# Group 0's mix loaded by whole feature tiles into the operand's low part, split there, and queued ahead of the residual

## The chip, the cores and the metric

The kernel runs on one core of a Trainium2 chip. The metric is the device time of one execution in microseconds (us). A core has five engines with queues of their own: TensorE (PE in the profile: matmuls; PEld: its weight loads), VectorE (DVE), ScalarE (ACT), GpSimd (POOL) and SyncE (SP). SyncE computes nothing here; it issues nearly all of the kernel's transfers (DMAs), in the order of its queue. Each engine works through its queue in order, and an instruction that waits holds up what stands behind it.

## What is computed

One layer of a streaming encoder for 1024 prompt frames and 32 sample frames, in float32. The input is modulated, projected to three groups of heads (mLSTM, FoX attention, gMLP), and their outputs are put side by side; this is the *mix*, 1024 features for each frame. It is projected once more, added to the residual and normalised; then comes a SwiGLU FFN with a second norm:

```python
mix = jnp.concatenate([hm.reshape(B, S, D_MLSTM).astype(dt),
                       hf.reshape(B, S, D_FOX).astype(dt), hg], axis=-1) @ w_o
x = _layer_norm(ALPHA * x + (1 + g1) * mix, ln1_g, ln1_b)
h = x * (1 + sc2) + sh2
y = (jax.nn.silu(h @ w_gate) * (h @ w_up)) @ w_down
x = _layer_norm(ALPHA * x + (1 + g2) * y, ln2_g, ln2_b)
```

## The kernel before

Everything is kept with features on the 128 partitions and frames along the free axis, so 1024 features are 8 feature tiles, counted k = 0 to 7. Frames fall into group 0 (frames 0 to 511) and group 1 (512 to 1055, the sample frames last). Large products are made in three passes to keep float32 precision: every operand is split into a high part, rounded to the type that TensorE takes at full rate (`F32R`), and a low part, the rest. `gemm` (lines 111 to 119) issues high x high, high x low and low x high into one PSUM bank. Making the split costs a cast on ScalarE and a subtraction, mostly on VectorE.

The mixers write their outputs to a scratch tensor in DRAM, `dmix[c]`, laid out as partition, feature tile, frame. In group 0, mLSTM writes tiles 0 and 1 (line 636, a store for each 128 frames), FoX tiles 2 to 5 (line 777, half a tile for each head), gMLP tiles 6 and 7 (line 669). The last mLSTM block and the last FoX head of group 0 end shortly before the output projection begins.

`run` then closes the mixers' SBUF pools and opens three others in their place (lines 1347 to 1351): `ph` with the operand tiles `ah` (high) and `al` (low), each 8 x 512 values a partition; `pz` with the residual `z0`, just as large; and `p2` with small work tiles, among them a ring `tmp` of four buffers of 272 values. By the sizes of the tiles in the closed pools, `al` lies over FoX's last key and query tiles, its values, its probabilities and one buffer of transposed probabilities; `z0` lies over the other transposed probabilities, FoX's output tiles and the start of the mLSTM tiles; `p2` over mLSTM tiles. A tile can be written when the tiles it lies over have been read for the last time.

The steps around the change, in the order of the source:

1. Line 1353, `wo_res(0)`: eight loads of the residual, one for each k, 128x512.
2. Line 1355, `wo_mix(0, KORDER[:6])`: the mix's tiles 2, 3, 4, 5, 0, 1. For each half of the group (frames 0 to 255, then 256 to 511) and each k: a load of 128x256 into a `tmp` buffer (line 932), a cast into `ah` (line 934), a subtraction into `al` (line 935).
3. Lines 1360 to 1368: the gMLP projections (`tm_unit`) and two q/k units (`fm_unit`, line 1368) for group 1; both kinds store their results to DRAM from SyncE.
4. Line 1370, `wo_mix(0, KORDER[6:])`: tiles 6 and 7, in the same way.
5. Lines 1374 and 1375, `wo(0, ...)`, once for each half: eight output blocks m of 24 matmuls. Each block loads a 128x1024 piece of `w_o` and splits it (lines 102 to 106); its products take the k in the order 2, 3, 4, 5, 0, 1, 6, 7. `sublayer_end` adds the product to the residual (line 975) and gathers the sums for the norm; after block 0 it also makes a pivot that later blocks need. Three PSUM banks (`pg`) serve these blocks.
6. Lines 1377 and 1378, the norm (`ln1`), which overwrites `ah` and `al` with the FFN's operand; lines 1379 and 1380, four more q/k units, which need nothing of the projection; then the FFN and, between its parts, the mixers of group 1.

The program is not issued in the order of the source. A scheduler places each instruction in its engine's queue by its own estimate of times, with the source's order as priority; an instruction whose inputs and buffers are ready may go ahead of earlier ones that wait. It draws up the order of the whole program at once (line 1576).

Of the kernel before, what the change touches and what calls it, by code (L numbers as in the profile page):

```python
# [10 lines left out]
ALU = mybir.AluOpType  # L11
# [54 lines left out]
def f(ap):  # L66
    return ap.bitcast(F32)


class Kernel:  # L70
# [855 lines left out]
    def wo_mix(self, c, ks):  # L926
        self.phase = f"wo{c}"
        nc = self.nc
        for a, b in MM[c]:
            for k in ks:  # L930
                r = self.t(self.p2, [P, 272], F32, "tmp", 4)[:, :b - a]
                self.load(r, self.dmix[c][:, k, a:b])
                h = self.hh[c][a][:, k, :b - a]
                nc.scalar.copy(h, r)
                nc.vector.tensor_tensor(self.hl[c][a][:, k, :b - a], r, f(h), ALU.subtract)
# [309 lines left out]
    def run(self):  # L1245
        nc, tc, d = self.nc, self.tc, self.d
# [103 lines left out]
        self.pz = self.pool("pz")  # L1350
        self.p2 = self.pada = self.pool("p2")
        self.hh, self.hl, self.z = {}, {}, {}
        self.wo_res(0, self.pz)
        self.operand(0, self.ph)
        self.wo_mix(0, self.KORDER[:6])
        def tail_ada():
            for u in rest:
                self.ada(u, self.wp, "raw", RAW, self.pg, "g")

        for i in range(4):  # L1360
            if i == ADAPOS:
                tail_ada()
            self.tm_unit(w2[3 + i % 2], 256, (self.evac_gv, self.evac_gmlp)[i % 2], range(4 * (i // 2), 4 + i // 2 * 5),
                         nc.gpsimd if GENG[i] else nc.vector)
        if ADAPOS == 4:
            tail_ada()
# [101 lines left out]
        for half, (a, b) in enumerate(LN[1][::-1]):  # L1468
# [6 lines left out]
            else:  # L1475
                h, l = (self.t(pb, [P, KT * 272], F32R, f"{x}{a}", 1) for x in ("ah", "al"))
# [111 lines left out]
```

## Time and profile before

| | us |
|---|---|
| runs of the kernel | 1397.95, 1398.54 (median), 1400.02 |
| the profiled execution | 1397.36 |
| its span, first to last instruction | 1395.6 |
| TensorE busy | 1346.8 |
| VectorE busy | 1034.0 |
| ScalarE busy | 641.6 |
| GpSimd busy | 258.7 |

The profile is one execution. In its lists, `out<-in` names the tiles an instruction writes and reads; a tile has the name of the stage that was being written when it was made, so the residual of group 0 is called `mlstm_z`, the operand's parts `mlstm_ah` and `mlstm_al`, the ring `wo_tmp`, and the scratch tensor `start_dmix`. `SPq` lines are issues of transfers in SyncE's queue: the time is that of the issue, not of the transfer. A row of waits reads: who waited, for whom, us in total, times, the longest. A row of a stretch reads: its bounds, its length, the busy time (with the count of instructions) of TensorE, its weight loads, VectorE, ScalarE and GpSimd, then the granted TensorE clock, the share of the DMA engines' time and the GB/s moved. A row of a group reads: line, engine, operation, tiles, shapes, count, busy us, mean ns of one, and the idle time of the engine ahead of them with what ended it. A row of the timeline reads: start, length, engine, line, instruction, count, and in brackets the idle time before it.

### The profile page before, as it was taken

The numbers are of one execution on the slowest core, as the hardware profiler recorded it, in microseconds if no ns is written. First come the engines' busy times: TensorE is split into PE (matmuls) and PEld (weight loads), VectorE is DVE, ScalarE is ACT, GpSimd is POOL, SyncE is SP. The second block draws the span as 40 slices with busy tenths as digits, with TensorE's granted clock in tenths as the row PEclk, the third lists the DMA queues.
The fourth block names the chain that finished last, engine by engine and source line by source line (L and its number), as shares of the span: only waits on it lengthen the run. The fifth ranks groups of instructions, "written<-read, shape, count | busy, mean of one in ns | idle before, by whom it ended". The sixth has DMA issues, their size and how long they took to land.

```text
span 1395.6 us, 25879 instructions
## 1 busy us (share of the span) xinstructions
PE 1346.8 (97%) x9651; PEld 1238.7 (89%) x9651; DVE 1034.0 (74%) x2198; ACT 641.6 (46%) x1257; POOL 258.7 (19%) x292
## 2 busy tenths in 40 slices
PE   7999999999979799999999999999999999999996
PEld 4899988899979778888887889899999999999996
DVE  5548646678779657777776766678997988888777
ACT  3313234445445444545544445344673544545355
POOL 0103200052146500000000000264620000000341
PEclk9999999999999899999999999999999999999998
DMA  9764577585755656444443342555597767563321
GB/s 360 255 219 134 171 234 210 176 253 168 225 174 158 186 174 178 128 131 138 137 131 85 100 119 83 198 153 139 157 237 202 204 174 199 149 174 112 101 91 65
DMA packets 134709, 233.09 MB, mean 167 GB/s; under 512 B 22436, under 2 KB 77356, under 8 KB 134584
## 3 DMA queue, kind: packets, MB, share of 16 engines
q1 hardware_dynamic: 129272, 221.34, 51.3%
q0 software_dynamic: 5168, 9.96, 4.6%
q8 instruction: 76, 1.25, 0.4%
q14 instruction: 49, 0.40, 0.1%
q10 hardware_dynamic: 144, 0.14, 0.0%
HBM read 197.50 MB, written 53.81 MB: 180 GB/s over the span
## 4 chain that ended last, share of the span: by engine, by line
PE 68%; DVE 4%; DMA 3%; issue 1%; ACT 1%; SPq 0%; POOL 0%; DVEq 0%; ACTq 0%
PE up_g L117 5%; PE up_g L118 5%; PE up_g L119 5%; PE dn_g L119 4%; PE dn_g L117 4%; PE dn_g L118 4%; PE sup_u L119 3%; PE sup_u L117 3%; PE sup_u L118 3%; PE wo_g L117 2%; PE wo_g L118 2%; PE wo_g L119 2%; PE sup_g L118 2%; PE sup_g L119 2%; PE sup_g L117 2%; PE fox_t L753 2%
## 5 line engine op out<-in xcount | busy, mean ns | idle before, releaser
L117 PE MATMUL up_g<-mlstm_ah,up_whi 128*128 128x512 f32 (+1 forms) x384 | 142.4, 371 | 4.3 <-ACT lna_tmp L996 3.4
L118 PE MATMUL up_g<-mlstm_al,up_whi 128*128 128x512 f32 (+1 forms) x384 | 142.8, 372 | 0.6 <-DVE mlstm_al L1001 0.6
L119 PE MATMUL up_g<-mlstm_ah,up_wlo 128*128 128x512 f32 (+1 forms) x384 | 142.2, 371 | 0.0
L284 PE MATMUL tm_g<-tm_whi,start_h1l 128*128 128x256 f32 (+1 forms) x384 | 110.0, 287 | 0.0
L282 PE MATMUL tm_g<-tm_whi,start_h1h 128*128 128x256 f32 (+1 forms) x384 | 109.6, 287 | 0.0
L283 PE MATMUL tm_g<-tm_wlo,start_h1h 128*128 128x256 f32 (+1 forms) x384 | 109.5, 286 | 0.0
L117 PE MATMUL fm_g<-start_h1h,fm_whi 128*128 128x256 f32 (+2 forms) x344 | 101.9, 301 | 4.7 <-DVE fm_qkl L367 2.0
L118 PE MATMUL fm_g<-start_h1l,fm_whi 128*128 128x256 f32 (+2 forms) x344 | 101.6, 295 | 0.2 <-DVE start_h1l L223 0.2
L119 PE MATMUL fm_g<-start_h1h,fm_wlo 128*128 128x256 f32 (+2 forms) x344 | 100.8, 294 | 0.0
L1120 ACT CAST sup_whi<-sup_raw 128x1024 fp32r<-128x1024 f32 x54 | 56.0, 1048 | 90.3 <-PE dn_u L118 46.7
L117 PEld LDWEIGHTS up_g<-mlstm_ah,up_whi 128*128 128x128 f32 x384 | 74.2, 193 | 16.6 <-ACT mlstm_ah L1000 3.5
L118 PEld LDWEIGHTS up_g<-mlstm_al,up_whi 128*128 128x128 f32 x384 | 74.3, 193 | 12.6 <-DVE up_actl L1054 0.8
L119 PEld LDWEIGHTS up_g<-mlstm_ah,up_wlo 128*128 128x128 f32 x384 | 74.4, 194 | 10.7
L105 ACT CAST up_whi<-up_raw 128x1024 fp32r<-128x1024 f32 x50 | 52.4, 1049 | 62.0 <-PE dn_g L118 22.5
L726 ACT ACTIVATE fox_p<-fox_s,fox_fmx 128x384 f32<-128x384 f32 (+2 forms) x96 | 55.1, 579 | 50.6 <-DVE fox_fmx L724 43.9
L1121 DVE TENSOR_TENSOR sup_wlo<-sup_raw,sup_whi 128x1024 fp32r<-128x1024 f32 x54 | 68.1, 1265 | 10.5 <-ACT sup_whi L1120 10.5
L117 PEld LDWEIGHTS fm_g<-start_h1h,fm_whi 128*128 128x128 f32 x344 | 65.4, 192 | 10.3 <-issue 2.9
L282 PEld LDWEIGHTS tm_g<-tm_whi,start_h1h 128*128 128x128 f32 x384 | 72.3, 189 | 1.9 <-issue 1.2
L106 DVE TENSOR_TENSOR up_wlo<-up_raw,up_whi 128x1024 fp32r<-128x1024 f32 x50 | 67.1, 1341 | 9.2 <-ACT up_whi L105 8.5
L284 PEld LDWEIGHTS tm_g<-tm_whi,start_h1l 128*128 128x128 f32 x384 | 72.3, 188 | 1.5 <-issue 1.2
L117 PE MATMUL dn_g<-up_acth,dn_whi 128*128 128x512 f32 (+2 forms) x200 | 73.5, 368 | 0.0
L118 PE MATMUL dn_g<-up_actl,dn_whi 128*128 128x512 f32 (+2 forms) x200 | 73.3, 368 | 0.0
(591 smaller groups left out, 4592.9 us busy)
## 6 DMA issues: line engine op xcount, KB each, us to landing
up_raw<-w_gu SPq DMA_DIRECT2D x50, 512.0 KB
dn_raw<-w_dn SPq DMA_DIRECT2D x28, 512.0 KB
ada_late<-w_ada SPq DMA_DIRECT2D x24, 512.0 KB
wo_raw<-w_o SPq DMA_DIRECT2D x24, 512.0 KB
sup_raw<-w_gu SPq DMA_DIRECT2D x20, 512.0 KB
start_dp<-w_gu SPq DMA_DIRECT2D x19, 512.0 KB
start_dp<-w_gu POOLq DMA_DIRECT2D x19, 512.0 KB, 7.9
sup_raw<-start_dp SPq DMA_DIRECT2D x18, 512.0 KB
```

Of the source, the lines that this page charges most:

```text
L105: nc.scalar.copy(hi[:, :w], raw[:, :w])
L106: (eng or nc.vector).tensor_tensor(lo[:, :w], raw[:, :w], f(hi[:, :w]), ALU.subtract)
L117: nc.tensor.matmul(ps, hi, xh(k), start=start and k == 0, stop=False)
L118: nc.tensor.matmul(ps, hi, xl(k), start=False, stop=False)
L119: nc.tensor.matmul(ps, lo, xh(k), start=False, stop=stop and k == n - 1)
L282: nc.tensor.matmul(ps[:, :ncol], xh, hi, start=k == 0, stop=False)
L283: nc.tensor.matmul(ps[:, :ncol], xh, lo, start=False, stop=False)
L284: nc.tensor.matmul(ps[:, :ncol], xl, hi, start=False, stop=k == 7)
L726: nc.scalar.activation(pr[:, lo:hi], banks[x][:, :hi - lo], AF.Exp, bias=mxs[:, 0:1], accum_out=sums[:, x:x + 1])
L753: nc.tensor.transpose(ps[:, c:c + P], probs[y][:, b * P:(b + 1) * P], self.ident)
L1120: nc.scalar.copy(h, x)
L1121: tt(l, x, f(h), ALU.subtract)
```

## The change

`wo_mix` gets a path of its own for group 0. For each k it loads the whole 128x512 tile into the slice of `al` that will hold its low part, casts from there into `ah`, and subtracts in place, so that `al` holds the low part afterwards. Both halves of the group are views of the same two tiles, so the projection reads them as before. The `tmp` ring is no longer used by group 0's mix; sixteen loads of 128x256 become eight of 128x512, and sixteen casts and subtractions become eight of each. The path of group 1 is untouched. In `run`, the residual's eight loads move behind the first six tiles of the mix.

```diff
@@ -926,6 +926,13 @@
     def wo_mix(self, c, ks):
         self.phase = f"wo{c}"
         nc = self.nc
+        if c == 0:
+            for k in ks:
+                h, l = self.hh[0][0][:, k], self.hl[0][0][:, k]
+                self.load(f(l), self.dmix[0][:, k])
+                nc.scalar.copy(h, f(l))
+                nc.vector.tensor_tensor(l, f(l), f(h), ALU.subtract)
+            return
         for a, b in MM[c]:
             for k in ks:
                 r = self.t(self.p2, [P, 272], F32, "tmp", 4)[:, :b - a]
@@ -1350,9 +1357,9 @@
         self.pz = self.pool("pz")
         self.p2 = self.pada = self.pool("p2")
         self.hh, self.hl, self.z = {}, {}, {}
-        self.wo_res(0, self.pz)
         self.operand(0, self.ph)
         self.wo_mix(0, self.KORDER[:6])
+        self.wo_res(0, self.pz)
         def tail_ada():
             for u in rest:
                 self.ada(u, self.wp, "raw", RAW, self.pg, "g")
```

`f` views a tile as plain float32, and `load` issues a transfer from SyncE's queue.

## The prediction

> **What bounds the kernel now.** I read the page's head first, then the table of waits of TensorE over the whole run, then busy times by stretch around the wait that the change touches, then the queue of SyncE.
>
> ```profile
> span 1395.6 us, 25879 instructions
> PE 1346.8 (97%) x9651; PEld 1238.7 (89%) x9651; DVE 1034.0 (74%) x2198; ACT 641.6 (46%) x1257; POOL 258.7 (19%) x292
> ```
>
> TensorE is busy 1346.8 of 1395.6 us, so it sets the end, and only its 48.8 us of idle time, with its slow matmuls, can be won. Which idle time is the change's? The waits of TensorE, longest first:
>
> ```profile
> PE ada_t L179 <- DMA ada_araw<-w_ada: 6.7, 2, 6.3
> PE wo_g L117 <- ACT mlstm_ah L934: 5.5, 1, 5.5
> ...
> PE wo_g L117 <- DVE mlstm_z L975: 1.3, 1, 1.3
> ...
> PE wo_g L119 <- DVE wo_wlo L106: 0.7, 1, 0.7
> ```
>
> The longest is the start of the kernel. The second longest, 5.5 us in one piece, is the output projection of group 0 waiting for line 934, which makes the high part of the mix. That is the line the change replaces. Around it, by stretch (us; then PE, weight load, DVE, ACT, POOL busy, granted clock, DMA share, GB/s):
>
> ```profile
> 379.10:386.10 7.00, 6.81 (x56) 6.56 (x55) 3.95 (x7) 2.84 (x7) 1.06 (x2) 1.00 0.95 291
> 386.10:391.30 5.20, 0.00 (x0) 0.00 (x0) 0.77 (x2) 1.11 (x4) 0.00 (x0) 0.67 0.64 222
> 391.30:394.60 3.30, 3.19 (x15) 3.19 (x16) 1.59 (x5) 1.21 (x5) 0.00 (x0) 0.50 0.32 84
> 394.60:401.10 6.50, 4.52 (x31) 3.86 (x31) 5.92 (x7) 3.71 (x5) 3.22 (x3) 0.99 0.46 144
> 386.10:401.10 15.00, 7.71 (x44) 7.06 (x45) 8.28 (x13) 6.02 (x11) 3.22 (x3) 0.77 0.49 158
> 401.10:441.00 39.90, 39.89 (x327) 39.74 (x328) 35.69 (x44) 20.57 (x34) 28.27 (x26) 1.00 0.60 179
> ```
>
> The last row is the undisturbed pace: 39.90 / 327 = 0.122 us for a matmul. The 44 matmuls of 386.1 to 401.1 would take 44 x 0.122 = 5.4 us; they took 15.0. So 15.0 - 5.4 = 9.6 us is everything that can be won here: 5.2 of standstill, 3.3 - 15 x 0.122 = 1.5 at half clock behind it, and 6.5 - 31 x 0.122 = 2.7 while the pipeline starts again (9.4 by parts; boundaries cut a record or two).
>
> Why is line 934 late? The queue of SyncE, in which every load and store of this stage goes out in order:
>
> ```profile
> 331.08 0.38 SPq L91 DMA_DIRECT2D start_dmix<-tm_gms  x1
> ...
> 345.28 0.35 SPq L87 DMA_DIRECT2D wo_raw<-w_o  x1
> ...
> 360.50 0.50 SPq L91 DMA_DIRECT2D start_dmix<-fox_fr  x1
> 361.97 0.37 SPq L91 DMA_DIRECT2D start_dmix<-mlstm_mixs  x1
> 362.84 3.67 SPq L87 DMA_DIRECT2D mlstm_z<-xT  x8
> 366.61 2.82 SPq L87 DMA_DIRECT2D wo_tmp<-start_dmix  x4
> ...
> 373.85 0.88 SPq L87 DMA_DIRECT2D wo_tmp<-start_dmix  x2
> ...
> 378.76 1.02 SPq L87 DMA_DIRECT2D wo_tmp<-start_dmix  x2
> ...
> 385.39 0.91 SPq L87 DMA_DIRECT2D wo_tmp<-start_dmix  x2
> 386.39 0.47 SPq L91 DMA_DIRECT2D o_kT<-fm_qkr  x1
> 386.96 4.82 SPq L87 DMA_DIRECT2D wo_tmp<-start_dmix  x4
> ```
>
> Eight residual loads go first. Then the mix comes in 16 pieces through a ring of four buffers (`tmp`): four at once, and every further pair only when the split of an earlier pair has freed its buffers. The last four pieces, which hold tiles 6 and 7, go out at 386.96, though their data was stored by 331.08 + 0.38. The chain of waits says the same:
>
> ```profile
> 366.61 5.51 DMA wo_tmp<-start_dmix
> ...
> 378.76 5.68 DMA wo_tmp<-start_dmix
> ...
> 386.96 3.97 DMA wo_tmp<-start_dmix
> ```
>
> A round of the ring costs a landing of 4.0 to 5.7 us, and TensorE, with three blocks begun in its three banks, can do no more without tiles 6 and 7.
>
> **The change, part by part.** *The ring goes.* A tile of 128x512 now lands in its own slice of `al`, so no load waits for a split. Each load waits for two things instead. One is that `al`'s place is free: it lies over buffers of the mixers' pool (the tail of FoX's keys and queries, its values, its probabilities and one transposed block), whose last reader is the last product of FoX head 7. The other is that its tile was stored.
>
> ```profile
> SPq L87 <- DMA start_dmix<-fox_fr: 0.4, 1, 0.4
> ...
> 358.17 0.46 PE L770 MATMUL fox_o<-fox_pth,fox_v 128*128 128x512 f32 x1
> 379.17 0.38 PE L117 MATMUL wo_g<-mlstm_ah,wo_whi 128*128 128x256 f32 x1
> ```
>
> So `al` is free at 358.17 + 0.46 = 358.6. Tiles 2, 3 and 4 (earlier heads), and 6 and 7, were stored before that. Tile 5 needs the store of 360.50. The residual, whose place lies over that store's source, waited for it (the first row) and started at 362.84, so such a store takes 2.3 us. Tiles 0 and 1 need the store of 361.97: 361.97 + 2.3 = 364.3. The first product that wants the mix starts at 379.17, and TensorE is busy without a gap until then.
>
> *Order past the residual.* At worst nothing lands early and all eight mix loads and eight residual loads are in the queue from 364.3: 16 x 0.262 MB = 4.2 MB. The rate of a full queue is in this row (share 0.99, 342 GB/s):
>
> ```profile
> 365.00:370.00 5.00, 5.00 (x43) 4.98 (x42) 3.03 (x5) 3.67 (x6) 0.00 (x0) 1.00 0.99 342
> ```
>
> 4.2 / 0.342 = 12.3 us, so the residual, now last, is in at 376.6. The eight mix loads, 2.1 MB, are in at 370.4. What is late next is the residual; its first use is the end of block 0, 24 matmuls after 379.17, at 382.1. Slack 5.5 us, so I cost the move at nothing. If that cover were gone, TensorE could still begin two more blocks in its other banks (2 x 24 x 0.122 = 5.9 us) before it stood.
>
> *Issue.* 16 issues become 8. Six of them now stand ahead of the eight residual issues (3.67 us), and ahead of what is queued after those: a gMLP store and load, and the stores of the two q/k units that TensorE runs until 379. Before, twelve of the sixteen mix loads stood among these and waited for buffers. The SP wait that is added, up to 364.3 for tiles 0 and 1, holds the residual 1.5 us longer than 362.84; nobody waits for that, by the slack above.
>
> *Splits.* Whole tiles were never split in this stage; the nearest rows are the same cast and subtraction on 128x512 in the FFN of group 1.
>
> ```profile
> L934 ACT CAST mlstm_ah<-wo_tmp 128x256 fp32r<-128x256 f32 x16 | 6.0, 405 | 13.9 <-DMA wo_tmp<-start_dmix 13.8
> L935 DVE TENSOR_TENSOR mlstm_al<-wo_tmp,mlstm_ah 128x256 fp32r<-128x256 f32 x16 | 7.9, 527 | 9.1 <-ACT mlstm_ah L934 9.1
> ...
> L1120 ACT CAST sup_w2h<-sup_w 128x512 fp32r<-128x512 f32 x18 | 11.0, 609 | 0.8 <-DMA sup_w<-w_gu 0.6 <-PE sup_u L118 0.2
> ...
> L1121 DVE TENSOR_TENSOR sup_w2l<-sup_w,sup_w2h 128x512 fp32r<-128x512 f32 x18 | 12.3, 682 | 0.0
> ```
>
> ScalarE: 16 x 0.405 = 6.5 us become 8 x 0.609 = 4.9. VectorE: 16 x 0.527 = 8.4 become 8 x 0.682 = 5.5. That the subtraction works in place has no row; bounds are 0.68 (as those rows) and 1.05 (two of the half-sized ones), at most 3 us over eight, and I take 0.68. Neither engine bounds here, so the path gets nothing from it directly. But ScalarE stood 13.8 us in front of these casts, with the casts of the projection's weights behind them in its queue; that frees the weights for blocks 1 to 3, and the 2.7 us of restart go with it.
>
> *The sum.* 5.2 + 1.5 + 2.7 = 9.4 us at most. I take 9.0, keeping 0.4 for the pivot of block 0 (the wait on line 975 above), which is part of any start. The rest of the run is TensorE-bound and slides forward. Against the profiled execution (1397.36 us, its span 1395.6) that is 1388.4; the median of the runs lies 1.2 above that execution, at 1398.54, so 1389.5 us.
>
> **The rivals.**
>
> *Half-way: the tiles still come late (1394.5 us).* DMA engines were 0.95 busy up to 386.1, and six pieces, 6 x 0.131 = 0.79 MB, had still to move. If the engines had been full whatever the order, these would take 0.79 MB / 0.291 = 2.7 us, with 1.3 us of split behind them: a hole of 4.0 us instead of 5.2. Of such a hole the half clock stays too, and the gain is 1.2 + 2.7 = 3.9, 1394.5 us. Is a hole that short punished? This trace has one:
>
> ```profile
> 472.23 0.36 PE L117 MATMUL up_g<-mlstm_ah,up_whi 128*128 128x256 f32 x1 [3.35 <-ACT lna_tmp L996]
> 474.00:478.00 4.00, 3.88 (x23) 3.68 (x22) 1.23 (x4) 3.02 (x9) 4.00 (x10) 0.67 0.61 161
> ```
>
> After 3.35 us of standstill the clock fell to 0.67, so holes from there up pay. The Trainium skill ("TensorE: Matmul & The Clock Gate", section "HAM oscillation — how this bites in real kernels") asks that TensorE never idle longer than about 3.4 us; by that alone this rival, with its hole cut to 3 us by splits that overlap, would keep full clock and gain 1.5 us more, while the trace puts the border at 3.35 or below. Against the rival: three to five tiles can move from 358.6 on, when the mixers' transfers are over.
>
> *The order is kept (1397.5 us).* The program's scheduler could leave the loads of tiles 6 and 7 behind the last store of the q/k units (386.39), as now. Then they land about when they do now, and only the 1 us of two further pieces is saved. Against: the projection's weights, which the source loads later still, were issued at 345.28, so the scheduler does draw loads forward once their buffer is free.
>
> *Slower (1402 us): the cover of the first norm is spent.* Four q/k units cover the norm after the projection:
>
> ```profile
> 436.00:463.00 27.00, 25.46 (x192) 24.57 (x192) 2.98 (x6) 3.36 (x7) 1.00 0.49 147
> ```
>
> Each is 25.46 / 4 = 6.4 us. The whole order after 345 us is drawn up anew, and if the scheduler puts units ahead of the projection, TensorE has less to do during the norm, and every unit so moved uncovers 6.4 us. From 9.0 / 6.4 = 1.4 units on it costs more than the change wins; with two it is 12.7 - 9.0 = 3.7 us slower, 1402 us. For it: the units' inputs are ready all along. Against: the source puts them behind the projection and the norm, and a mix that is ready sooner leaves fewer gaps to fill with them.
>
> **How the numbers follow.** Forecast 0.55, 1389.5 us, with its own range 1386 to 1392.5 (all 9.6 won, the run like the fastest of those shown, and some luck of order, to 6 won). Half-way 0.15. Order kept 0.10. Slower 0.20. The bound of what can be told apart is 0.2%, 2.8 us: faster is below 1395.7, slower above 1401.3. So faster 0.70, same 0.10, slower 0.20. The range 1386 to 1400 holds all but the slower case.
>
> **What would show it.** In the changed profile: eight mix loads, no line 932 loads of group 0 in `tmp`, most issued before the residual and several between 358 and 365; the wait of the projection's products on the high part gone; TensorE busy from 345 to about 450 with clock 1.00; the norm's start near 427 instead of 436. The sum is wrong if a wait on the residual or on weights stands where the mix's stood. The step to the end is wrong if the norm starts 9 us sooner and the kernel doesn't end so. Half-way shows as a hole of 3 to 4 us near 386, the order kept as loads of tiles 6 and 7 behind the last q/k store, the slower case as q/k units ahead of the projection and idle TensorE during the norm.

## The result, and the profile after

Medians of the runs: 1399.88 us before (1397.53 to 1401.07, 8 runs), 1389.95 us after (1384.43 to 1395.11, 8 runs). The ratio is 0.9934, with an interval of 0.9914 to 0.9953. The changed kernel, measured again later beside the kernel before (run e8 below), gave 1388.72 against 1396.87 us, 0.9943 (0.9922 to 0.9964). The forecast was 1389.5 us.

The profiled execution of the changed kernel took 1389.64 us. The head of its page, for comparison with 1346.8 busy of a span of 1395.6 us before:

```profile
span 1387.8 us, 25846 instructions
PE 1344.1 (97%) x9651; PEld 1236.2 (89%) x9651; DVE 1030.4 (74%) x2190; ACT 641.0 (46%) x1249; POOL 260.2 (19%) x292
```

TensorE's idle time fell from 48.8 to 43.7 us, its busy time by 2.7 us (in this stage no matmul runs at a low clock any more). The same stretches as before the change, in the same columns:

```profile
379.10:386.10 7.00, 7.00 (x56) 6.70 (x56) 4.59 (x9) 3.14 (x5) 0.97 (x2) 1.00 1.00 312
386.10:391.30 5.20, 5.20 (x46) 5.20 (x44) 3.85 (x5) 3.02 (x6) 4.59 (x7) 1.00 0.89 295
...
386.10:401.10 15.00, 15.00 (x128) 15.00 (x127) 13.65 (x16) 8.03 (x13) 14.07 (x14) 1.00 0.67 210
```

Where 44 matmuls ran in 15.0 us, 128 run now, at clock 1.00. SyncE's queue after (issues, with their times):

```profile
360.81 0.37 SPq L91 DMA_DIRECT2D start_dmix<-mlstm_mixs  x1
361.27 2.80 SPq L87 DMA_DIRECT2D mlstm_al<-start_dmix  x6
364.12 6.35 SPq L87 DMA_DIRECT2D wo_z<-xT  x8
370.93 0.38 SPq L91 DMA_DIRECT2D start_dmix<-tm_gms  x1
371.61 0.33 SPq L87 DMA_DIRECT2D tm_gvn<-start_dvn  x1
...
372.93 0.32 SPq L87 DMA_DIRECT2D mlstm_al<-start_dmix  x1
...
374.31 0.32 SPq L87 DMA_DIRECT2D mlstm_al<-start_dmix  x1
...
375.60 0.49 SPq L87 DMA_DIRECT2D wo_raw<-w_o  x1
...
376.67 0.94 SPq L87 DMA_DIRECT2D wo_raw<-w_o  x2
```

(`wo_z` is the residual, `mlstm_z` before.) Six tiles go out ahead of the residual, tiles 6 and 7 at 373 and 374 instead of 387, and three loads of `w_o` right behind them. The residual's eight issues take 6.35 us where they took 3.67, though they need nothing of the mix. SyncE's own waits from 355 to 400 us say what held them:

```profile
SPq L87 <- DMA mlstm_al<-start_dmix: 2.5, 3, 1.2
```

Three of them stood until an earlier transfer, a mix tile, had landed; what makes them wait is taken up at e9. TensorE's waits from 345 to 475 us:

```profile
PE ada_g L179 <- DVE up_sil L1059: 4.1, 1, 4.1
PE up_g L117 <- DVE fm_qkl L367: 2.7, 1, 2.7
PE fm_g L117 <- ACT tm_gms L665: 1.4, 1, 1.4
```

The wait on the high part is gone. A small new one is there: line 665, gMLP's copy out of its bank, now stands in ScalarE's queue behind four of the new casts. The splits cost what the rows of the other stage had said: 0.616 us a cast (0.609 in the prediction), 0.684 us for the subtraction in place (0.68). Both rows give shortest/median/longest in ns:

```profile
L933 ACT CAST mlstm_ah<-mlstm_al x8: 602/616/622, 365.0 to 378.3; 128x512 fp32r<-128x512 f32 x8
L934 DVE TENSOR_TENSOR mlstm_al<-mlstm_al,mlstm_ah x8: 668/684/693, 365.9 to 379.8; 128x512 fp32r<-128x512 f32 x8
```

**A measure that is sharper than the time.** Single executions of one kernel differ by 10.7 us (the range above) and by up to 14.3 (the kernel before, beside e9 to e12: 1390.44 to 1404.72), more than the change is worth. Much of that lies outside the stage. Up to gMLP's third store (358.37 in the queue of before) the program has the same instructions in the same order on every engine in all the kernels of this study, and yet that store came between 356.9 and 363.0 us in the fourteen profiled executions. So each kernel's stage is measured from that store in its own trace, to the last matmul of the output projection. One execution each, in us:

| kernel | first output product | last output product | median of runs, ratio (interval) |
|---|---|---|---|
| before | 20.8 | 77.5 | 1399.88, 1397.53, 1396.87, 1397.65 |
| changed | 22.2 | 69.2 | 1389.95, 0.9934 (0.9914 to 0.9953) |
| changed, again (e8) | 21.8 | 69.2 | 1388.72, 0.9943 (0.9922 to 0.9964) |
| e1 order only | 20.6 | 75.1 | 1394.13, 0.9981 (0.9966 to 0.9996) |
| e2 whole tiles only | 21.6 | 69.5 | 1390.04, 0.9949 (0.9931 to 0.9967) |
| e3 ring of eight | 24.4 | 78.2 | 1395.16, 0.9980 (0.9962 to 0.9998) |
| e4 changed, `qkl` 3 | 22.0 | 68.9 | 1390.11, 0.9943 (0.9923 to 0.9963) |
| e5 pieces in place | 22.7 | 77.2 | 1396.27, 0.9996 (0.9983 to 1.0008) |
| e6 whole tiles, ring | 22.7 | 75.7 | 1397.38, 0.9998 (0.9981 to 1.0015) |
| e7 late split, `qkl` 3 | 21.8 | 68.7 | 1389.74, 0.9942 (0.9922 to 0.9962) |
| e9 pieces, mix early | 24.5 | 73.4 | 1393.34, 0.9963 (0.9944 to 0.9981) |
| e10 pieces, weights early | 26.7 | 74.8 | 1393.98, 0.9973 (0.9959 to 0.9988) |
| e11 pieces, both early | 24.5 | 72.7 | 1394.43, 0.9976 (0.9960 to 0.9991) |
| e12 whole tiles, both early | 23.3 | 69.8 | 1393.17, 0.9966 (0.9950 to 0.9982) |

Two executions of the changed kernel agree within 0.1 us in the last product (0.4 in the first), where their times differ by 3.7 us; of every other kernel there is one trace. The stage became 8.3 us shorter (77.5 to 69.2), which is the gain of the medians (9.9 and 8.2 us) within their spread.

### The profile page after: what moved, and what is told of

Same layout as the page of the kernel before. It is cut to its first block, busy times and chain, and to the rows that moved or that the text cites. A ratio compares the mean times of both kernels' runs of the same rounds, so it can differ in the third digit from the quotient of the medians.

```text
span 1387.8 us, 25846 instructions
## 1 busy us (share of the span) xinstructions
PE 1344.1 (97%) x9651; PEld 1236.2 (89%) x9651; DVE 1030.4 (74%) x2190; ACT 641.0 (46%) x1249; POOL 260.2 (19%) x292
## 4 chain that ended last, share of the span: by engine, by line
PE 69%; DVE 4%; DMA 2%; ACT 1%; issue 1%; POOL 0%; SPq 0%; DVEq 0%; ACTq 0%
PE up_g L117 5%; PE up_g L118 5%; PE up_g L119 5%; PE dn_g L119 4%; PE dn_g L117 4%; PE dn_g L118 4%; PE sup_u L119 3%; PE sup_u L117 3%; PE sup_u L118 3%; PE wo_g L118 2%; PE wo_g L119 2%; PE wo_g L117 2%; PE sup_g L118 2%; PE sup_g L119 2%; PE sup_g L117 2%; PE fox_t L753 2%
## 5 line engine op out<-in xcount | busy, mean ns | idle before, releaser
L119 PEld LDWEIGHTS up_g<-mlstm_ah,up_wlo 128*128 128x128 f32 x384 | 74.6, 194 | 10.7
L982 DVE SCALAR_TENSOR_TENSOR wo_z<-dn_g,start_mod,wo_z 128x512 f32<-128x512 f32 (+4 forms) x120 | 60.3, 521 | 21.1 <-PE dn_g L119 20.5
L118 PE MATMUL dn_g<-up_actl,dn_whi 128*128 128x512 f32 (+2 forms) x200 | 73.4, 368 | 0.0
```

The lines of the kernel that those rows point to most:

```text
L118: nc.tensor.matmul(ps, hi, xl(k), start=False, stop=False)
L119: nc.tensor.matmul(ps, lo, xh(k), start=False, stop=stop and k == n - 1)
L982: self.lastz = self.nc.vector.scalar_tensor_tensor(z[:, m, x:y], ps[:, x - a:y - a], g[i], z[:, m, x:y], ALU.mult, ALU.add)
```

## The experiments

The theory of the prediction was that the ring of four buffers made the mix late, and that neither the residual's place nor the number of transfers mattered. e1 to e4 ran on one chip, e5 to e8 on a second, e9 to e12 on a third, with the kernel before beside them (1397.53, 1396.87 and 1397.65 us).

**e1: only the order.** The kernel before, with the residual's loads behind the first six tiles.

```diff
-        self.wo_res(0, self.pz)
         self.operand(0, self.ph)
         self.wo_mix(0, self.KORDER[:6])
+        self.wo_res(0, self.pz)
```

> Only the order is changed: the residual's eight loads go behind the first six tiles of the mix, which still come in 16 pieces through the ring of four buffers. Theory ring (the loads wait for buffers, a landing of 4 to 6 us for each round): the ring starts 3.8 us sooner (362.8 instead of 366.6) and keeps its rounds, so the 5.5 us wait shrinks but stays: 1395 to 1398 us, with a wait of the projection on line 934 of 1 to 4 us. Theory order (the 2 MB of residual ahead in the queue delay the mix): nearly all of the gain, 1388 to 1392 us. Theory size (fewer and larger transfers): no gain, 1398 to 1401 us.

Measured: 0.9981, a stage 2.4 us shorter. The wait on the high part is gone, but another has its place (TensorE's waits, 345 to 475 us):

```profile
PE wo_g L117 <- ACT wo_whi L105: 3.2, 1, 3.2
...
PE wo_g L119 <- DVE wo_wlo L106: 0.7, 1, 0.7
```

The queue shows why:

```profile
383.43 1.06 SPq L87 DMA_DIRECT2D wo_tmp<-start_dmix  x2
384.53 14.68 SPq L87 DMA_DIRECT2D wo_raw<-w_o  x7
```

The loads of the weights from the third block on now stand behind the last pieces of the mix. In the kernel before, three of them stood among the pieces, at 373 and 375 us.

**e2: only the whole tiles.** The changed kernel with the residual first, as before.

```diff
+        self.wo_res(0, self.pz)
         self.operand(0, self.ph)
         self.wo_mix(0, self.KORDER[:6])
-        self.wo_res(0, self.pz)
```

> Only the whole tiles are changed: eight loads straight into the low part, but the residual goes first, as before. Theory ring: no load waits for a buffer, the six tiles follow the residual at once and land by about 376, tiles 6 and 7 by 380: the hole is gone, 1389 to 1392 us. Theory order: the mix still lands behind 2 MB of residual and the hole stays, 1396 to 1400 us. Theory size: 1389 to 1392 us, like ring; the third run tells these two apart.

Measured: 0.9949, stage 69.5 us. This part alone brings what the change brings; by these two traces the residual's place is worth 0.3 us of stage.

**e3: only more buffers.** The kernel before with eight buffers, four of them in another pool.

```diff
-            for k in ks:
-                r = self.t(self.p2, [P, 272], F32, "tmp", 4)[:, :b - a]
+            for i, k in enumerate(ks):
+                p, tag = (self.p2, "tmp") if c or i % 2 else (self.pr, "mixr")
+                r = self.t(p, [P, 272], F32, tag, 4)[:, :b - a]
...
```

> The kernel before with a ring of eight buffers instead of four for the pieces of group 0's mix (every second piece takes a buffer of a ring of its own); same 16 pieces, same splits, residual first. Theory ring: half the rounds, tiles 6 and 7 go out about 8 us sooner, the 5.5 us wait is gone: 1389 to 1393 us. Theory order: the residual is still ahead, 1397 to 1400 us. Theory size: still 16 small transfers and 16 small splits, 1397 to 1400 us.

Measured: 0.9980, and a stage no shorter (78.2). The wait on the high part fell from 5.5 to 0.8 us, and others came:

```profile
PE tm_g L655 <- DMA tm_gvn<-start_dvn: 2.1, 1, 2.1
PE wo_g L117 <- ACT wo_whi L105: 1.2, 1, 1.2
PE wo_t L860 <- DVE mlstm_z L976: 1.1, 1, 1.1
```

The first is new: `tm_gvn` is a small operand of gMLP's last frames that goes out to DRAM and is loaded again, by SyncE, behind the pieces.

**e4: three `qkl` buffers.** The changed kernel; `qkl` is a tile of the q/k units, with which VectorE had waited 4.3 us for a store during the norm.

```diff
-            lo = self.t(self.sm, [P, 272], F32R, "qkl", 2)
+            lo = self.t(self.sm, [P, 272], F32R, "qkl", 3)
```

> The changed kernel with three buffers instead of two for the low part of the q/k units, whose stores VectorE waited for in the middle of the norm (4.3 us in the changed kernel's profile, 2.1 before). Theory give-back (the 2 us that the changed kernel lost again in the norm come from VectorE standing behind that store): 1386 to 1388 us, no wait of VectorE on that store during the norm, and runs that lie closer together. Rival (the norm is held by the loads of the FFN's weights or by GpSimd): as the changed kernel, 1389 to 1391 us, with the wait moved to another row.

Measured: 1390.11 us, not the 1386 to 1388 expected. TensorE still waited 3.2 us for `fm_qkl` and 3.4 us for `up_sil` in the norm. Nothing won.

**e5: no ring, but pieces.** The changed kernel with 128x256 pieces, sixteen of them, straight into `al` and split there.

```diff
-            for k in ks:
-                h, l = self.hh[0][0][:, k], self.hl[0][0][:, k]
-                self.load(f(l), self.dmix[0][:, k])
+            for x, y in MM[0]:
+                for k in ks:
+                    h, l = self.hh[0][0][:, k, x:y], self.hl[0][0][:, k, x:y]
+                    self.load(f(l), self.dmix[0][:, k, x:y])
```

> The changed kernel, but each tile of group 0's mix is still loaded, cast and subtracted in two pieces of 128x256; the pieces go straight into the operand's low part, so there is no ring. If the ring of four buffers was what made the mix late: within 2 us of the changed kernel run beside it (near 1390 us), no standstill of TensorE at the first output block, all sixteen mix loads issued without a wait for a split. If the size of the transfers or the count of splits mattered (16 x 0.405 us of casts instead of 8 x 0.6): 1394 to 1397 us, with a hole of 3 us or more before the products of the first block.

Measured: 0.9996. Without any ring the gain is gone. TensorE's waits and SyncE's queue:

```profile
PE wo_g L117 <- ACT wo_whi L105: 4.1, 1, 4.1
PE wo_g L119 <- DVE wo_wlo L106: 0.9, 1, 0.9
PE tm_g L655 <- DMA tm_gvn<-start_dvn: 0.7, 1, 0.7
```

```profile
364.91 5.64 SPq L87 DMA_DIRECT2D mlstm_al<-start_dmix  x12
370.60 4.02 SPq L87 DMA_DIRECT2D wo_z<-xT  x8
375.23 0.38 SPq L91 DMA_DIRECT2D start_dmix<-tm_gms  x1
375.86 0.68 SPq L87 DMA_DIRECT2D tm_gvn<-start_dvn  x1
...
382.45 0.94 SPq L87 DMA_DIRECT2D mlstm_al<-start_dmix  x2
...
387.93 0.58 SPq L87 DMA_DIRECT2D mlstm_al<-start_dmix  x1
388.55 10.49 SPq L87 DMA_DIRECT2D wo_raw<-w_o  x5
```

Twelve pieces went out in one go (5.64 us for twelve, 0.47 each), so nothing waited for a split. But the scheduler put the last pieces and all further weights at the end of the q/k stores, and TensorE stood for weights that were asked for at 388.55.

**e6: whole tiles, but a ring.** The changed kernel's eight tiles through two buffers of 128x512.

```diff
-                self.load(f(l), self.dmix[0][:, k])
-                nc.scalar.copy(h, f(l))
-                nc.vector.tensor_tensor(l, f(l), f(h), ALU.subtract)
+                r = self.t(self.pr, [P, 512], F32, "mixr", 2)
+                self.load(r, self.dmix[0][:, k])
+                nc.scalar.copy(h, r)
+                nc.vector.tensor_tensor(l, r, f(h), ALU.subtract)
...
```

> The changed kernel, but its eight whole tiles go through a ring of two buffers of 128x512 (as many bytes as the ring of four before), and are split from there into the operand. If the ring was the cause: four rounds of two tiles at 4 to 5 us a round, the last tiles late again, 1393 to 1397 us, a wait of the output projection on the high part or the weights of 2 us or more, clock below 0.9 between 379 and 401 us. If the size of the transfers was: within 2 us of the changed kernel, no such wait.

Measured: 0.9998, stage 75.7, a wait on the high part of 2.6 us; the last two tiles were asked for at 388.56. With a ring, whole tiles do not help either, as the ring theory said (the clock stayed at 1.00, other than expected).

**e7: later splits and three `qkl` buffers.** In the source, the first six tiles are loaded where they were and split behind the gMLP projections.

```diff
-        self.wo_mix(0, self.KORDER[:6])
+        self.wo_mix(0, self.KORDER[:6], "load")
         self.wo_res(0, self.pz)
...
+        self.wo_mix(0, self.KORDER[:6], "split")
         for h in range(QD, PRE):
```

> The changed kernel with two more edits: the casts and subtractions of the first six mix tiles stand behind the gMLP projections in the source (their loads stay where they are), and the ring qkl of the q/k units has three buffers instead of two. If the give-back behind the change is made of two waits of their own (1.4 us of TensorE on the gMLP copy, 2 us in the norm's cover): the wait on tm_gms is gone, VectorE's wait on the store of qkl falls below 2.6 us, and the median is 1386.5 to 1388.5 us, under the changed kernel beside it by 1.5 us or more. If what the norm costs is set by VectorE's chain and only changes its name: the same as the changed kernel within 1.5 us, with the waits on up_sil and up_g as long as there.

Measured: 1389.74 us beside 1388.72 for the changed kernel. The scheduler drew the casts forward to the places that they had, so the first edit did nothing, and the wait on `tm_gms` stayed at 1.1 us. VectorE's wait on the store of `qkl` was 3.3 us from 345 to 475 us (5.7 in e8), but all of it lay behind 420 us, where e8 had 2.7, and TensorE's waits in the norm kept their size (3.8 us for `lna_tmp` in both, 2.6 and 2.2 for `up_sil`). The time is that of the second case of the expectation; that VectorE's chain sets these waits, as it said, is not shown apart. What line 665's place costs was not tried.

**e8: the changed kernel again.**

> The changed kernel itself, beside the three above and the kernel before on the same chip. 1388 to 1392 us, 7 to 9.5 us under the kernel before. If single runs differ by the start of the program, its first output product comes more than 2 us earlier or later than 379.36 us while the stage behind it, from the store of gMLP's last tile to the last product of the output projection, keeps 69 us within 1.5.

Measured: 1388.72 us; the stage keeps 69.2 us. In the trace, the first output product came at 378.67, 0.7 us earlier than in the first trace, so this pair alone doesn't show the spread of the start.

**e9 to e11: the places in SyncE's queue.** All three are e5 with one or both of these edits. The first calls tiles 6 and 7 earlier, and so puts their loads right behind the residual; the second raises the priority of the first five weight loads (200 in e11 and e12, 500 in e10), and so puts three of them ahead of the q/k stores.

```diff
         for i in range(4):
+            if i == 2:
+                self.wo_mix(0, self.KORDER[6:])
...
-        self.wo_mix(0, self.KORDER[6:])
...
-            w = self.weights(self.d["w_o"][m], KT, P, eng)
+            if c == 0 and cuts[0][0] == 0 and m < 5:
+                with self.tc.high_priority(200):
+                    w = self.weights(self.d["w_o"][m], KT, P, eng)
+            else:
+                w = self.weights(self.d["w_o"][m], KT, P, eng)
```

> The run of sixteen pieces in place, but tiles 6 and 7 of the mix are called in the source behind the second gMLP projection, so that their four loads stand right behind the residual in SyncE's queue, ahead of the q/k stores; the w_o loads of blocks 2 to 15 still come at the end of those stores. Theory A (the mix's last tiles were still late): 1389 to 1391 us, no wait on weights. Theory B (the weights of block 2 are what is late, since their load stands behind the mix pieces and the q/k stores): no gain over that run, 1394 to 1397 us, a wait of the output projection on line 105 of 3 us or more. Theory C (pieces as such cost): 1394 to 1397 us without a wait on weights of that size.

> The run of sixteen pieces in place, but the weights of the first five output blocks have a higher priority in the scheduler, so that three more w_o loads stand right behind the residual; tiles 6 and 7 of the mix still stand behind the q/k stores. Theory A (the mix's last tiles late): 1393 to 1396 us, a wait on line 934 of 2 us or more. Theory B (weights late): 1389 to 1391 us, no wait of 2 us at the output projection. Theory C (pieces as such): 1394 to 1397 us with neither.

> Sixteen pieces in place with both edits: the loads of tiles 6 and 7 and three more w_o loads stand ahead of the q/k stores. If the place in SyncE's queue is what the change bought (A or B): 1388 to 1391 us, TensorE busy from 379 to 401 us at clock 1.00, as in the changed kernel. If the pieces cost by their number (C): 1394 us or more.

Measured: stages of 73.4, 74.8 and 72.7 us, where e5 had 77.2 and the changed kernel 69.2. None met theory A or B with its full gain; e11's 1394.43 us is where theory C, a price on the number of pieces, had put it. The waits at the output projection on the mix and on weights are gone in all three (theory B had expected e9 to keep one), and a wait earlier in the stage has taken their place. From e9, e10 and e11 in this order:

```profile
PE tm_g L655 <- DMA tm_gvn<-start_dvn: 1.7, 1, 1.7
PE tm_g L663 <- DVE tm_vhl L658: 1.0, 1, 1.0
```

```profile
PE tm_g L655 <- DMA tm_gvn<-start_dvn: 3.2, 1, 3.2
PE tm_g L663 <- ACT fm_qkh L366: 1.0, 1, 1.0
```

```profile
PE wo_g L117 <- ACT tm_gms L665: 1.1, 1, 1.1
PE tm_g L663 <- DVE tm_vhl L658: 1.0, 1, 1.0
PE tm_g L655 <- DMA tm_gvn<-start_dvn: 0.9, 1, 0.9
```

The chain of waits of e9 leads back from there into SyncE's queue (start, us, what; each `SPq L87` is one issue):

```profile
363.01 0.42 SPq L87
...
370.61 0.43 SPq L87
371.08 6.62 DMA wo_z<-xT
377.76 3.57 DMA tm_gvn<-start_dvn
381.38 0.82 PE tm_g L655 x8
382.42 0.66 DVE tm_vhl L658 x3
383.21 0.39 PE tm_g L663 x2
383.60 0.51 PE wo_g L117
```

Seventeen issues in a row (363.01 to 370.61), the landing of a residual load (the eighteenth, issued at 371.08), and only then is `tm_gvn` asked for, at 377.76: 18.8 us behind gMLP's third store. In the changed kernel it was 371.61, 14.4 us behind that store. Its landing takes 3.6 us, and TensorE needs it at 379.6.

Why should `tm_gvn` wait for a residual load, of which it needs nothing? SyncE's waits of e9, from 355 to 400 us:

```profile
SPq L87 <- DMA wo_z<-xT: 2.1, 5, 0.7
```

That residual load is the eighth transfer ahead of `tm_gvn` in SyncE's queue. In all fourteen traces SyncE's transfers signal their landing on eight semaphores in turn, none of its 821 to 829 transfers went out before the last one on its semaphore had landed whole, and the first load of `tm_gvn` behind gMLP's third store left SyncE just when the eighth transfer ahead of it had landed: within 0.14 us in thirteen of them, 1.1 us later in e1. So in these programs at most eight of SyncE's transfers are under way at once, and a small load behind a burst waits for landings, not only for issues of 0.47 us. A piece of 128x256 takes one of the eight places, as a whole tile does. That the eight places are what the pieces lose by is argued from this, not tried: no run has more of them.

**e12: whole tiles and both edits.**

> The changed kernel with both edits. If its stage is already without a hole: 1388 to 1391 us, nothing won within 0.2%. If there is still something to win ahead of the norm (the 1.4 us on the gMLP copy among it): 1386 to 1388 us.

Measured: 1393.17 us, above both expectations, though its stage is nearly the changed kernel's (69.8 us) and TensorE's only waits in it are 1.0, 0.9 and 0.3 us. The profiled execution was the slowest of its twelve (1394.41). Its trace was at gMLP's third store at 362.66, 5.5 us later than the first trace of the changed kernel, with the same program up to there. Whether that late start belongs to this kernel or to that execution, one trace can't say; the 3.2 us above the first median of the changed kernel (4.5 above the second, both taken elsewhere) stay open. No version beat the changed kernel.

## Why the prediction was right in time, and where its cause fell short

*What bounds, and what can be won: right.* The output projection was to give at most 9.6 us. From its first to its last matmul it took 435.9 - 379.2 = 56.7 us before and 426.4 - 379.4 = 47.0 us after, 9.7 us less; the clock is 1.00 and the weights of blocks 1 to 3 are in time. The norm began at 426.5 (427 was forecast).

*The ring as the cause: half of it.* The step "the ring goes, so no load waits for a split" is true of the changed kernel, and e6 shows that a ring costs most of the gain even with whole tiles (75.7 us of stage). But taking the ring away, with the new order, wins 0.3 us (e5). The sentence that failed is the one on issues: "16 issues become 8", with nothing put down for it, since nobody waited for the residual. Others stand in SyncE's queue behind those issues: the weights of the third block and `tm_gvn`. Behind gMLP's third store, `tm_gvn` was asked for after 12.1 us in the kernel before, where the ring kept twelve pieces back, after 14.4 in the changed one, and after 15.0 in e5 and 18.8 in e9. With sixteen issues that no ring keeps back, one or the other comes late, wherever the mix itself stands (e5, and e9 to e11). By stage lengths, from e5's 77.2 us: the better places in the queue are worth 2.4 to 4.5 us (e9 to e11), and the halved number of transfers the other 3.5 to 5.6, down to 69.2. The closest pair is e11 and e12, with the same two edits: 72.7 and 69.8 us of stage, `tm_gvn` after 17.9 and 15.7. Their medians, 1394.43 and 1393.17 us, are too close to show that difference in the time. The splits are halved with the transfers, which was not tried apart; the chain of e9 goes by issues and a landing, and holds no split of the mix. What was argued from one wait in the profile was the first of several that stood almost equally late: e1, e3 and e5 each removed or shrank it and met the next one. That the time came out right is luck to this extent: the change also halves the transfers, and by the prediction's reasoning alone e5 would have had the same forecast, 7 us under its 1396.27.

*That three to five tiles "can move from 358.6 on": wrong, at no cost.* None was issued before 361.27, since SyncE's queue had the stores of 359.48 and 360.81 ahead of them, and tiles 6 and 7, stored long before, went out at 373 and 374. The slack that the prediction worked out for the residual covered that.

*The order past the residual at nothing: right* (e2 and the changed kernel, 69.5 and 69.2 us). *The splits: right in size*, as the rows above show, but not wholly off the path: `tm_gms` stood behind four of the casts, and TensorE waited 1.4 us for it, which the sum had put at nothing.

*"The rest slides forward": right on the whole.* In the first trace the new wait on `tm_gms` took 1.4 us and the stretch from the last output product to group 1's first FoX score product (line 819) grew from 63.5 to 65.2 us; in the second trace it was 62.9, so that loss is not a fixed price. From that FoX product to the end, the first trace and the trace before took 896.2 us each; over all fourteen it was 893.3 to 897.7.

*The rivals.* "Order kept" was refuted by the queue; "slower" did not come, as the q/k units behind the projection stayed there. "Half-way" was refuted too, with its premise: the DMA engines' share was 1.00 from 379 to 386 us, fuller than before, and the tiles were in time all the same, because they had been asked for earlier. Its bound for a punished hole is taken up below.

## What to carry to other kernels

Before a wait is put down to one cause, look at what stands next in the same issuing queue: with one engine issuing all transfers, each issue (0.47 us here) and each wait, for a buffer or for the landing of the eighth transfer ahead, delays everything behind it, and removing one late load can uncover the next. The Trainium skill ("Perfetto Trace Analysis", section "What "DMA-bound" means") lists the issuing engine's queue, solid with issues, as a bound of its own beside the DMA engines, with larger descriptors as the remedy; e9's seventeen issues in a row and the shorter stage of whole tiles (69.8 us in e12, 72.7 in e11) agree; behind those issues e9's queue is not solid, it waits for landings. Fewer, larger transfers that need no buffer to come free did here what neither fewer transfers nor freer buffers did alone. Where executions vary in their start by more than the effect, measure the stage from a point that all kernels share.

## What the runs showed of the hardware

Outside the changed stage the start varied most, by 6.1 us (356.9 to 363.0) against 4.4 behind FoX's first score product of group 1 (893.3 to 897.7). With the same instructions in the same order, TensorE's waits of the FoX heads on the loads of one operand took 1.7 us in one trace and 5.8 in another (20 to 357 us; the kernel before, then e2):

```profile
PE fox_s L717 <- DMA fox_qp<-start_dql: 1.7, 1, 1.7
```

```profile
PE fox_s L717 <- DMA fox_qp<-start_dql: 5.8, 3, 2.7
```

The granted clock after a standstill did not follow its length alone. At one point of the program, with 128x256 matmuls on both sides, TensorE stood for 1.97 us in the kernel before and for 1.97 us in e5. The matmul behind the standstill, and the three microseconds that follow it, in the kernel before and then in e5:

```profile
140.82 0.39 PE L117 MATMUL fm_g<-start_h1h,fm_whi 128*128 128x256 f32 x1 [1.97 <-DVE fm_qkl L367]
...
142.00:145.00 3.00, 3.00 (x17) 3.00 (x16) 2.91 (x4) 1.38 (x3) 2.91 (x5) 0.52 0.30 81
```

```profile
142.16 0.39 PE L117 MATMUL fm_g<-start_h1h,fm_whi 128*128 128x256 f32 x1 [1.97 <-DVE fm_qkl L367]
...
143.00:146.00 3.00, 3.00 (x28) 3.00 (x27) 2.90 (x4) 1.72 (x3) 2.85 (x4) 1.00 0.42 122
```

The same standstill was followed by 0.52 in one execution and by 1.00 in the other. Elsewhere 2.64 us left the clock at 1.00 (e6, at 393.65), and 2.07 us (e3, at 377.63) and 3.17 us (e1, at 390.39) were followed by 0.58 and 0.50. All 23 standstills of 2.95 us or more behind the first 10 us of the fourteen traces were followed by about 0.5 within 2.5 us. So between 1.97 and 2.95 us the length alone does not tell which standstill is punished. The prediction's bound of 3.35 us or below holds, but its own trace had a punished standstill of 1.97 us; its half-way rival's holes of 3 to 4 us lie where all were punished here. The Trainium skill ("TensorE: Matmul & The Clock Gate", section "HAM oscillation — how this bites in real kernels") asks for idle stretches no longer than about 3.4 us; 1.97 us in the kernel before and 3.17 us in e1 were punished, so that length is not safe here. What besides the length decides was not tried.
